# An encoder trunk on one core: the rate at which retention and attention steps are mixed into the weight products

## Chip, cores and metric

One core of a Trainium2 chip runs the kernel, in one launch. The metric is device microseconds of one execution; three runs of the kernel before took 2622.9 to 2623.79 us, median 2623.04 us.

## What is computed

The reference runs an encoder of two layers (DEPTH = 2) over two batches, of 512 and 256 tokens (together T = 768), with the same weights; D_MODEL is 1024. Cut to what matters:

```python
def encoder_layer(x, ...):
    h = rmsnorm(x, norm_mix)
    proj = h @ w_in
    z, xbc, dt_raw, rq, rk, rv, rg, nq, nk, nv, gates = jnp.split(proj, splits, axis=-1)
    ...
    y = bidir_scan(cm, bm, xh * dt_f[..., None], ...)          # the SSD mixer
    o_ssd = rmsnorm(y ... * jax.nn.silu(z), ssd_norm)
    ...
    yr = bidir_scan(q, k, v, la_f, v, la_b)                    # retention, 4 heads
    o_ret = rmsnorm(yr) ... * jax.nn.silu(rg)
    o_na = neighborhood_attention(nq, nk, nv, na_rpb)          # attention, 8 heads
    gates = jax.nn.sigmoid(gates + gate_bias)
    merged = gates[:, :, 0] * (branches[0] @ w_branch[0])      # o_ssd
    for i in range(1, N_BRANCH):
        merged = merged + gates[:, :, i] * (branches[i] @ w_branch[i])   # o_ret, o_na
    x = x + merged @ w_out
    h2 = rmsnorm(x, norm_ffn)
    ...                                                        # gated MLP with a convolution
    return x
```

## The kernel before

**Arithmetic.** Every fp32 value that goes into a large product is split into two parts (`hi` and `lo`, type fp32r), and three matmuls make one product. Weights come by DMA (`wraw`, L197), ScalarE writes `whi` (L206) and VectorE `wlo` (L207). For the projections to nq and nk and to the gates two blocks of 128 output columns are made at once with seven products in place of eight (`pair_products`, L500): each of the seven is four steps of three matmuls with 384 columns (`prod`, L489 to L494), so a pair has 84 matmuls. Its sums are formed on the way from PSUM by ScalarE and VectorE (`soon`, L498) in the tiles `pt`, `pv` and `pg`.

**Stages of a layer.** Norm and the projections for z, dt and xbc; four projections by token tiles (`t_job`) beside which the SSD mixer runs; then sixteen pairs: four for nq and nk (L1178), ten for gate columns in the pool `mix` (L1191) and two more for gates in the pool `br` (L1217). They are called the first four pairs and gate pairs 1 to 12 here. Then the branch products, the output projection and the MLP.

**Side work.** The SSD mixer, retention (`ret`, L924) and attention (`na`, L1052) are Python generators. Each `yield` ends a step; a step holds some loads, some small matmuls and transposes and the ScalarE and VectorE work behind them. `side.pump(p)` adds p to a sum and runs one step for every whole 1.0 in it. `pair_products` calls it six times, after each of its first six products, and the seventh product, put off into the next pair by `pending()`, calls it once more (L565). `t_job` pumps the SSD mixer with 2.7 after each of its 24 token tiles.

- Retention has 27 steps: one of constants, 8 for the chunk states and their sums, and three for each of the six chunks of 128 tokens (scores, output, norm). Its loads `rk`, `rv`, `rqk`, `rgt` share three buffers (`ld2`); the output tile `ro` has one.
- Attention has 56 steps: for each of four head pairs four units of 128 prompt queries and two of sample queries, two steps each (scores with softmax; transposes and values), and two steps that normalise and store. The first step of a head pair loads keys (`kh`, `kl`), for every other head pair also the values (`nv`, many small DMAs), then `q` and `bias`. The scores are `nsc`, the transposed weights `npT`, the output `npo` and `no`.

Each of the two has a pool of its own, opened and closed inside the generator, over the same memory, so attention's tiles wait for retention's. The pool `br` of the last two gate pairs (merged, `oT0h`, `oT0l`, three buffers `g`, two `ot`) is laid over `mix` and attention's pool in the same way; its tiles wait tile by tile. In bytes of a partition, in the order of first use: `mix` 19072; attention `kh` 4096, `kl` 4096, `nv` 7168, `q` 4096, `bias` 4096, `nsb` 6144, `npT` 4096, `no` 2048, and for the sample `kh` 2048, `kl` 2048, `nv` 2048; `br` 24576 + 12288 + 12288, then `g` 3 x 3072, `ot` 2 x 2048.

**Order.** All DMAs are issued by SP, in one queue. The order of instructions on each engine is made when the program is built, by a planner (L1395, `schedule_with_timeline_sim=True`): it takes what is ready by its own reckoning of time, earlier emitted instructions first, and the ones inside `soon` as if they had been emitted 100 earlier. On the chip every engine then goes through its queue in that order. So the place of a `pump` call sets a step's rank, not its exact place.

The lines that the change touches are L1145, where `PUMP` is set, and L1192, where the ten gate pairs pass it on.

Of the kernel before, what the change touches and what calls it, by code (L numbers as in the profile page):

```python
# [283 lines left out]
def body(tc, nc, a, depth=DEPTH):  # L284
# [25 lines left out]
    for n, op in (("ident", OP.is_equal), ("U", OP.is_ge), ("Y", OP.is_le)):  # L310
        m = cst.tile([P, P], F32, name="mask" + n)
# [4 lines left out]
    for n, op in (("V", OP.is_lt), ("W", OP.is_gt)):  # L316
        m = cst.tile([P, P], F32R, name="maskr" + n)
# [254 lines left out]
    def pending():  # L572
        while late:
            late.pop(0)()
# [13 lines left out]
    def layer(l, x_in, prev_x):  # L588
# [5 lines left out]
        m = mctx.enter_context(tc.tile_pool(name=f"mix{l}", bufs=1, reuse_waits="tile"))  # L594
# [547 lines left out]
            nctx.close()  # L1142


        PUMP = 1.6  # L1145

        def pair(pool, tag, bufs, pump, evac):
            vg = [pool.tile([P, T], F32, name=n, tag=tag, bufs=bufs) for n in ("pv", "pg")]
            tmp = pool.tile([P, T], F32, name="pt", tag=tag, bufs=bufs)
            pair_products(*vg, tmp, lambda j: evac(j, vg[j]), pump=pump)  # L1150

        def nq_evac(i, r):

            s = mt([P, T], "nst", "cv", 6)
            src = r[:, :TP].rearrange("p (r c) -> p r c", c=GW)
            if i < 4:
                act(s[:, :TP].rearrange("p (b r c) -> p r b c", b=4, c=16),
                    src.rearrange("p r (b c) -> p r b c", c=16), AF.Copy, scale=0.125)
                act(s[:, TP:T], r[:, TP:T], AF.Copy, scale=0.125)
            else:  # L1160
                act(s[:, 0:64].rearrange("p (r c) -> p r c", c=8), src[:, :, 0:8], AF.Copy)
                act(s[:, 64:448].rearrange("p (b r c) -> p r b c", b=3, c=16),
                    src[:, :, 8:56].rearrange("p r (b c) -> p r b c", c=16), AF.Copy)
                act(s[:, 448:512].rearrange("p (r c) -> p r c", c=8), src[:, :, 56:64], AF.Copy)
                act(s[:, TP:T], r[:, TP:T], AF.Copy)
            hi, lo = (mt([P, T], n, "cv", 6, F32R) for n in ("nhi", "nlo"))
            act(hi, s, AF.Copy)
            tt(lo, s, hi.bitcast(F32), op=OP.subtract)
            for s_ in range(2):
                h, rw = 2 * (i % 4) + s_, slice(s_ * 64, s_ * 64 + 64)  # L1170
                scr, parts = (nq_scr, (hi, lo)) if i < 4 else (nk_scr, (hi, hi))
                for j, part in enumerate(parts):
                    nc.sync.dma_start(scr[h, j * 64:j * 64 + 64], part[rw].bitcast(F32))
            if i >= 4:
                nc.sync.dma_start(nkl_scr[i - 4], lo.bitcast(F32))

        side.add(ret())
        for i in range(0, 8, 2):  # L1178
            pair(m, "cv", 6, PUMP, lambda j, r, i=i: nq_evac(i + j, r))
        side.add(na())  # L1180


        def gates(i, pool, tag, bufs, pump):
            def evac(j, g):
                act(g, g, AF.Tanh, bias=gbh[:, i + j:i + j + 1], scale=0.5)
                nc.sync.dma_start(gate_scr[i + j], g)

            pair(pool, tag, bufs, pump, evac)

        NG1 = 20  # L1190
        for i in range(0, NG1, 2):  # L1191
            gates(i, m, "cv", 6, PUMP)  # L1192
        pending()
        side.drain()
        mctx.close()
# [180 lines left out]
    for l in range(depth):  # L1376
        prev = layer(l, x_in, prev)
        x_in = x_scr
# [20 lines left out]
```

## Time and profile before

| | |
|---|---|
| median of 3 runs | 2623.04 us |
| the profiled execution | 2621.23 us |
| its span, first to last instruction | 2619.5 us |
| TensorE busy | 2560.9 us (98%) |
| VectorE busy | 1906.4 us (73%) |
| ScalarE busy | 1150.0 us (44%) |
| mean granted clock of TensorE | 0.995 |

The stages lie, by the copies of each pair's first product (`pt`, L498): the first four pairs and gate pairs 1 and 2 from 299.3 to 416.8 us, gate pairs 3 to 6 to 528.9, 7 to 9 to 573.1, 10 and 11 to 607.5. In layer 1 the same marks are 1600.2, 1715.2, 1828.4 and 1872.6.

How to read it: TensorE's own ends are modelled and matmuls overlap, so a stretch in which it is busy throughout isn't free of loss by that alone; the spacing of starts tells more. What a wait of another engine costs is seen only where TensorE idles too.

### The profile page before, as it was taken

What the parts mean: (1) busy time and instruction counts of PE and PEld (TensorE: products, weight loads), DVE (VectorE), ACT (ScalarE), POOL (GpSimd) and SP (SyncE); (2) the same over time, 40 slices, a digit from 0 to 9 for tenths busy, and PEclk for the clock granted to TensorE, in tenths of its full rate; (3) what the DMA queues carried; (4) which work ended last, traced back from release to release, by engine and by line L of the source; (5) the groups of instructions that cost most, each with busy time, mean ns of one, the idle gap of its engine ahead of it and who ended that gap; (6) DMA issues with size and microseconds to landing.
All of it is one profiled execution on the core that took longest, in us unless ns stands there. A gap on an engine that the chain in (4) does not pass through costs nothing.

```text
span 2619.5 us, 37552 instructions
## 1 busy us (share of the span) xinstructions
PE 2560.9 (98%) x14290; PEld 2352.9 (90%) x14290; DVE 1906.4 (73%) x3204; ACT 1150.0 (44%) x1946; POOL 86.5 (3%) x130
## 2 busy tenths in 40 slices
PE   8999999999999999999999999999999999999998
PEld 8878898998888999999998789989998899999997
DVE  6748876565658887888867588755656598888887
ACT  5434464643225433333453445655432353333433
POOL 0002100000000000000000011100000000000000
PEclk9999999999999999999999999999999999999999
DMA  7356577736521222222353565786474222222222
GB/s 247 107 167 210 193 229 221 222 130 225 161 87 57 73 73 66 64 73 73 126 181 118 161 224 177 231 238 196 135 229 150 73 81 66 64 65 73 73 65 89
DMA packets 168900, 359.65 MB, mean 137 GB/s; under 512 B 16080, under 2 KB 62480, under 8 KB 168720
## 3 DMA queue, kind: packets, MB, share of 16 engines
q1 hardware_dynamic: 168720, 357.25, 43.3%
q8 instruction: 113, 1.85, 0.3%
q14 instruction: 67, 0.55, 0.1%
HBM read 276.87 MB, written 80.31 MB: 136 GB/s over the span
## 4 chain that ended last, share of the span: by engine, by line
PE 80%; DMA 9%; DVE 5%; ACT 2%; issue 2%; SPq 1%; POOL 1%; DVEq 0%; POOLq 0%; ACTq 0%
PE acc L492 12%; PE acc L493 12%; PE acc L494 12%; PE dn L1343 5%; PE dn L1342 5%; PE dn L1341 5%; PE acc L366 4%; PE acc L368 4%; PE acc L367 4%; PE acc L389 3%; PE acc L388 3%; PE acc L390 3%; DMA cw<-cum_scr 2%; PE wo L390 2%; PE wo L388 2%
## 5 line engine op out<-in xcount | busy, mean ns | idle before, releaser
L206 ACT ACTIVATE whi<-wraw 128x1024 fp32r<-128x1024 f32 (+2 forms) x444 | 432.6, 984 | 644.4 <-DMA wraw<-wp 162.7
L207 DVE TENSOR_TENSOR wlo<-wraw,whi 128x1024 fp32r<-128x1024 f32 (+2 forms) x444 | 499.9, 1131 | 166.5 <-ACT whi L206 163.1
L492 PE MATMUL acc<-hTh,whi 128*128 128x384 f32 x1216 | 413.6, 341 | 5.5 <-DVE pg L498 2.6
L493 PE MATMUL acc<-hTl,whi 128*128 128x384 f32 x1216 | 410.9, 338 | 5.0 <-DVE hTl L435 5.0
L494 PE MATMUL acc<-hTh,wlo 128*128 128x384 f32 x1216 | 409.4, 338 | 0.0
L492 PE MATMUL acc<-Eh,whi 128*128 128x384 f32 x912 | 309.0, 340 | 1.3 <-DVE pv L498 1.3
L494 PE MATMUL acc<-Eh,wlo 128*128 128x384 f32 x912 | 306.9, 338 | 0.0
L493 PE MATMUL acc<-El,whi 128*128 128x384 f32 x912 | 306.9, 337 | 0.0
L492 PEld LDWEIGHTS acc<-hTh,whi 128*128 128x128 f32 x1216 | 229.4, 189 | 9.7 <-ACT pt L498 3.5
L493 PEld LDWEIGHTS acc<-hTl,whi 128*128 128x128 f32 x1216 | 229.4, 189 | 7.5 <-DVE hTl L435 6.0
L494 PEld LDWEIGHTS acc<-hTh,wlo 128*128 128x128 f32 x1216 | 229.0, 188 | 0.4
L389 PE MATMUL acc<-wlo,hTh 128*128 128x512 f32 (+1 forms) x576 | 210.1, 366 | 2.6 <-DVE wlo L207 2.6
L388 PE MATMUL acc<-whi,hTh 128*128 128x512 f32 (+1 forms) x576 | 209.1, 364 | 2.2 <-ACT whi L206 1.5
L390 PE MATMUL acc<-whi,hTl 128*128 128x512 f32 (+1 forms) x576 | 209.3, 365 | 0.0
L1342 PE MATMUL dn<-wlo,ah 128*128 128x512 f32 x528 | 207.6, 393 | 0.0
L1343 PE MATMUL dn<-whi,al 128*128 128x512 f32 x528 | 201.9, 394 | 0.0
L1341 PE MATMUL dn<-whi,ah 128*128 128x512 f32 x528 | 200.5, 393 | 0.0
L492 PEld LDWEIGHTS acc<-Eh,whi 128*128 128x128 f32 x912 | 171.4, 188 | 3.6 <-DVE pv L498 2.7
L366 PE MATMUL acc<-hTh,whi 128*128 128x256 f32 (+1 forms) x512 | 174.1, 340 | 0.0
L1356 DVE TENSOR_TENSOR x<-x,dn 128x512 f32<-128x512 f32 x168 | 111.8, 684 | 85.0 <-PE dn L1343 84.9
L368 PE MATMUL acc<-hTh,wlo 128*128 128x256 f32 (+1 forms) x512 | 173.1, 338 | 0.0
L367 PE MATMUL acc<-hTl,whi 128*128 128x256 f32 (+1 forms) x512 | 173.0, 338 | 0.0
(277 smaller groups left out, 4769.3 us busy)
## 6 DMA issues: line engine op xcount, KB each, us to landing
wraw<-wp SPq DMA_DIRECT2D x284, 512.0 KB
g<-gate_scr SPq DMA_DIRECT2D x48, 384.0 KB
cw<-cum_scr SPq DMA_DIRECT2D x48, 256.0 KB
xt<-xbc_scr SPq DMA_DIRECT2D x20, 512.0 KB
bias<-nab SPq DMA_DIRECT2D x40, 256.0 KB
gate_scr<-pg SPq DMA_DIRECT2D x24, 384.0 KB
gate_scr<-pv SPq DMA_DIRECT2D x24, 384.0 KB
ot<-o_scr SPq DMA_DIRECT2D x36, 256.0 KB
```

What stands on the lines that cost most here:

```text
L206: self.nc.scalar.activation(hi[:, :n], r, AF.Copy)
L207: self.nc.vector.tensor_tensor(lo[:, :n], r, hi[:, :n].bitcast(F32), op=OP.subtract)
L366: mm(o, wh[:, k, :], rh, start=(k == 0), stop=False)
L388: mm(o, hT[0][:, k, ts_], wh[:, cs], start=(k == 0), stop=False)
L389: mm(o, hT[0][:, k, ts_], wl[:, cs], start=False, stop=False)
L390: mm(o, hT[1][:, k, ts_], wh[:, cs], start=False, stop=(k == NK - 1))
L492: mm(o, w[0][:, k, :], r[0][:, k, :], start=first and k == 0, stop=False, skip_group_check=True)
L493: mm(o, w[0][:, k, :], r[1][:, k, :], start=False, stop=False, skip_group_check=True)
L494: mm(o, w[1][:, k, :], r[0][:, k, :], start=False, stop=k == 3, skip_group_check=True)
L1341: mm(ps, ah[:, tsl], wh[:, cs], start=(j == 0), stop=False)
L1342: mm(ps, ah[:, tsl], wl[:, cs], start=False, stop=False)
L1343: mm(ps, al[:, tsl], wh[:, cs], start=False, stop=(j == n - 1))
```

## The change

Two rates replace one. `PUMP` was 1.6 for the first four pairs and for ten gate pairs. Now it is 27/28 for the first four pairs (28 calls, 27 steps of retention) and `PUMP_G` = 56/66 for the ten gate pairs (70 calls, 56 steps of attention). `side.add(ret())`, `side.add(na())`, `side.drain()` and the 0.5 of the last two gate pairs stay where they are.

```diff
-        PUMP = 1.6
+
+        PUMP, PUMP_G = 27 / 28, 56 / 66
...
         NG1 = 20
         for i in range(0, NG1, 2):
-            gates(i, m, "cv", 6, PUMP)
+            gates(i, m, "cv", 6, PUMP_G)
         pending()
         side.drain()
```

## Rows read from the trace of the kernel before

**Rows 1.** The page, busy time and share of the span of each engine.
```profile
PE 2560.9 (98%) x14290; PEld 2352.9 (90%) x14290; DVE 1906.4 (73%) x3204; ACT 1150.0 (44%) x1946; POOL 86.5 (3%) x130
```
**Rows 2.** Windows: length, busy us (instructions) of PE, PEld, DVE, ACT, POOL; clock, DMA, GB/s.
```profile
170.00:299.00 129.00, 129.00 (x646) 108.88 (x646) 97.62 (x201) 55.35 (x120) 23.35 (x20) 0.99 0.56 184
299.30:416.80 117.50, 113.89 (x734) 112.66 (x733) 91.12 (x137) 72.60 (x161) 7.76 (x12) 1.00 0.68 211
416.80:528.90 112.10, 104.57 (x720) 102.15 (x719) 63.89 (x189) 61.90 (x153) 0.00 (x0) 0.98 0.79 230
528.90:573.10 44.20, 44.20 (x255) 44.20 (x254) 28.98 (x40) 19.05 (x25) 0.00 (x0) 1.00 0.36 125
...
1600.20:1715.20 115.00, 112.83 (x729) 111.90 (x728) 90.77 (x137) 72.89 (x161) 8.21 (x12) 1.00 0.70 216
1715.20:1828.40 113.20, 105.87 (x720) 104.12 (x720) 63.99 (x189) 61.85 (x153) 0.00 (x0) 0.97 0.78 228
1828.40:1872.60 44.20, 44.20 (x254) 44.20 (x254) 29.02 (x40) 19.03 (x24) 0.00 (x0) 1.00 0.37 125
```
**Rows 3.** Timeline of TensorE: start, duration; first and last of ten matmuls.
```profile
432.07 0.52 PE L494 MATMUL acc<-Eh,wlo 128*128 128x384 f32 x1
...
434.95 0.34 PE L494 MATMUL acc<-hTh,wlo 128*128 128x384 f32 x1
```
**Rows 4.** Waits of TensorE, 299 to 417: total us, times, longest.
```profile
PE acc L492 <- DVE pg L498: 1.6, 1, 1.6
PE qT L330 <- ACT qd L1005: 1.1, 1, 1.1
PE rst L977 <- DMA rv<-rv_scr: 0.8, 1, 0.8
```
**Rows 5.** The same waits in layer 1, 1600 to 1715.5.
```profile
PE rst L977 <- DMA rv<-rv_scr: 1.0, 1, 1.0
PE acc L492 <- DVE pg L498: 1.0, 1, 1.0
```
**Rows 6.** Waits of TensorE, 417 to 529.
```profile
PE nsc L1101 <- DMA q<-nq_scr: 6.2, 2, 3.7
PE nsc L1101 <- issue: 0.9, 1, 0.9
PE nsc L1101 <- DVE nmx L1109: 0.4, 1, 0.4
```
**Rows 7.** The same in layer 1, 1715.5 to 1829.
```profile
PE nsc L1101 <- DMA q<-nq_scr: 5.1, 2, 3.0
PE nsc L1101 <- DVE no L1130: 0.9, 1, 0.9
PE nsc L1101 <- DVE nmx L1109: 0.7, 1, 0.7
PE nsc L1101 <- DVE wlo L207: 0.7, 1, 0.7
```
**Rows 8.** Timeline of SP's queue where retention ends and attention begins.
```profile
409.91 0.32 SPq L1040 DMA_DIRECT2D o_scr<-ro  x1
...
414.68 9.95 SPq L1070 DMA_DIRECT2D nv<-nv_scr  x10
424.67 0.44 SPq L1092 DMA_DIRECT2D q<-nq_scr  x1
```
**Rows 9.** Timeline of VectorE; in brackets its idle time and what ended it.
```profile
408.43 0.69 DVE L1038 TENSOR_TENSOR ry<-ry,rs 128x512 f32<-128x512 f32 x1 [3.71 <-POOL rs L419]
```
**Rows 10.** Timeline: the last scores of attention and its last store, layer 0.
```profile
513.37 0.28 PE L1102 MATMUL nsc<-kl,q 128*128 128x256 f32 x1
...
526.21 0.38 SPq L1139 DMA_DIRECT2D o_scr<-no  x1
```
**Rows 11.** Timeline: a load of retention and the matmul that waited for it.
```profile
320.49 0.33 SPq L970 DMA_DIRECT2D rv<-rv_scr  x1
...
325.66 0.60 PE L977 MATMUL rst<-rv,kg 128*128 128x128 f32 x3 [0.77 <-DMA rv<-rv_scr]
```

## The prediction

> **What bounds the kernel now.** I read the page first: TensorE is busy 98% of the span [rows 1], so the change can only give back what TensorE loses between its instructions. Then the windows by stage [rows 2]: where the span exceeds TensorE's busy time, it idled. In layer 0 the stretch in which retention runs (299.3 to 416.8) idles 117.50 - 113.89 = 3.6 us, the one in which attention runs (416.8 to 528.9) 112.10 - 104.57 = 7.5 us, and the three gate pairs behind it, which have no side work, idle 0 (44.20 of 44.20: 14.7 us for a pair, 0.175 us for each of its 84 matmuls). Layer 1 has 2.2 us, 7.3 us and 0. Together 20.6 us.
>
> To this comes a slower clock. The granted clock is 0.98 and 0.97 in the two attention stretches and 1.00 in the pairs behind them [rows 2]: behind the longest idle stretch, of 3.7 us, nine matmuls were issued from 432.07 to 434.95, 0.32 us apart, TensorE's lower level (1.2 GHz instead of 2.4) [rows 3]. That cost 2.88 - 9 x 0.175 = 1.3 us; scaled by the missing clock (0.02 to 0.03) layer 1 lost some 2.0 us (an estimate). So the two stretches lose about 24 us in the two layers, 0.9% of the run. No more can be won.
>
> The views of who waited for whom, by stretch, say for what. In retention, layer 0: 1.6 us for `pg` on VectorE, 1.1 us for `qd`, 0.8 us for a load of `rv` [rows 4]; layer 1: 1.0 us for `rv` and 1.0 us for `pg` [rows 5]. In attention, layer 0: 6.2 us for two loads of `q`, the longer 3.7 us, and 1.3 us for small things [rows 6]; layer 1: 5.1 us for two loads of `q`, the longer 3.0 us, and 2.3 us [rows 7].
>
> **The change, part by part.** It adds and removes no instruction. All 14290 matmuls stay, and so do the DMAs; what moves is where the 27 retention and 56 attention steps stand in the order in which the planner takes instructions. There are 28 calls of `side.pump` by the first four pairs and 70 by the ten gate pairs. At 1.6 a call retention was handed out after 17 calls (27/1.6) and attention after 35 (56/1.6, five gate pairs); now it takes 28 and 66. A step is moved with its loads and stores, all on SP's queue, past the weight loads (L197) and the stores of `nq_evac` and the gates (L1186). Waits are added only by tiles that a later pool takes over (below).
>
> *Retention.* Its work already runs past where it was handed out: the store of its last `ro` goes out at 409.91 [rows 8], in gate pair 2, though it was handed out by pair 3 of the first four. Its loads share three buffers (`ld2`), so buffers and not the rate set its pace, and I expect its end at about the same place, 400 to 425. What can go are the waits of two chunks that run close together. The 1.6 us wait for `pg` comes from there: VectorE stood 3.71 us at L1038, waiting for POOL's `rs` [rows 9], with the pair's own instructions queued behind. The `pg` and `qd` waits sum to 1.6 + 1.0 + 1.1 = 3.7 us; at the earliest all go, at the latest none. I take half, **-1.8 us**, as nothing says which. The `rv` waits (1.8 us) belong to the state chunks, whose loads come one buffer ahead before and after: 0.
>
> *The start of attention.* Its pool takes over retention's memory, so its first loads follow retention's end: `kh` behind 409.91, then the small loads of `nv`, of which ten hold SP's queue for 9.95 us, then `q` at 424.67 [rows 8], for which TensorE waits the 3.7 and 3.0 us. The first step issues the same burst wherever it stands, so I keep these 6.7 us and their clock loss: **0**, with -6.7 - 2.3 = -9 us as the good end.
>
> *The rest of attention.* The other waits are 7.5 - 3.7 = 3.8 us in layer 0 and 7.4 - 3.0 = 4.4 us in layer 1, with some 1 us of clock loss 9.2 us. They come with density: twelve loads of `q`, the bias, key and value tiles of a layer go through within some 112 us, and the DMA engines are busy 0.79 there, against 0.36 in the pairs behind [rows 2]. The change spreads the same bytes over 112 + 44 us. The nearest row for even spreading is the SSD stage: its 58 steps are pumped at 2.7 a call over 22 of 24 calls, and behind its start, from 170 to 299, TensorE idles 0 of 129.00 us beside them [rows 2]. But attention starts late (its memory), so about five of its 24 units are handed out by then and run as densely as now. I take three quarters: **-6.9 us**, ends 0 and -9.2.
>
> *The end of attention.* By the tile sizes in the code the pool of the last two gate pairs puts its three `g` buffers where `npT`, `no` and the sample's `kh` and `kl` lie. Before, the last `no` was stored at 526.21 [rows 10], some 47 us ahead of gate pair 10, so that nobody waited for it. Now the last step is handed out at the fourth call of gate pair 10. From the last `nsc` to that store took 526.21 - 513.37 = 12.8 us [rows 10]. That `nsc` is now handed out two products earlier than the last step, and from that step to the copy of gate pair 11's first product (`pt`, L498) are four products, then two more that don't need the copy: eight in all, 8 x 12 x 0.175 = 16.8 us. It just fits, with the landing of the store. I take **+0.8 us** a layer, ends 0 and +6.
>
> *Pairs 7 to 9* lose their quiet: 0 by the SSD row; VectorE is busy 0.66 of them and ScalarE 0.43 [rows 2], which leaves room.
>
> Sum: -1.8 + 0 - 6.9 + 1.6 = **-7.1 us**. The profiled execution took 2621.2 us (span 2619.5 and 1.7 around it), so 2614.1 by it; the median of the runs shown is 2623.0, 1.8 above it, so the median should be **2616 us** (-0.27%).
>
> **The rivals.**
>
> *The rate isn't what these steps wait for (no change).* Retention's pace is set by buffers, the start of attention by the burst, and the backlog behind it runs as before. Then only half of the smaller waits go: (3.7 + 9.2)/4 = 3 us, **2620 us**. For it: retention ended two pairs behind its handing out. Against it: the SSD row. The Trainium skill ("Perfetto Trace Analysis", Optimization Strategy) says that the same gap repeating on the engine that should be saturated can mean that there isn't enough SBUF or PSUM for the next tile. By that rule the gaps are bound to buffers and stay, whatever the rate. The trace agrees for retention's start and for attention's; for the second wait for `q` it shows a busy DMA instead.
>
> *Loads lose their lead (slower).* Handed out at twice the rate, attention's loads went out as soon as a buffer was free, well ahead of their matmuls. Handed out evenly, a unit's `q` is issued next to the matmul that needs it. If the planner thinks loads faster than they are, TensorE meets the matmul early, every time. The nearest row: `rv`, issued at 320.49, let TensorE go on at 325.66 only, after 0.77 us of idling [rows 11]. At 0.8 us for each of 2 x 12 loads that is +19.2, less the -8.7 of the gains: +10.5, **2633.5 us**; it is slower than before from 0.4 us a load on. For it: the waits in [rows 4 to 7] that a load ends. Against it: the SSD stage, which loads its tiles in the same manner and idles 0.
>
> *The tail of attention holds gate pair 11 (about 2627 us).* If attention lags by one unit (some 5 us) more than above, TensorE idles 5 us a layer and loses 1.3 us of clock behind it: +12.6 - 8.7 = +3.9. For it: attention ran one to two gate pairs late before. Against it: that lag came from the density that goes.
>
> *The burst goes too.* If the planner puts the first `nsc` later, -9 comes on top with all of the smaller waits: -22, **2601 us**. Nothing in the trace speaks for it but the room.
>
> **How the numbers follow.** Forecast 0.42 (2611 to 2620), rate without effect 0.28, lead lost 0.14, tail 0.06, burst gone 0.10. About 0.2% (5.2 us) is what a measurement can tell from no change: faster is below 2617.8, slower above 2628.3. Faster: 0.37 of the forecast's 0.42, 0.10 from the burst and 0.03 from the first rival, 0.50. Slower: 0.14, 0.03 of the tail and 0.03 of the first rival with a worse order of queues, 0.20. Same: the remaining 0.30. The range goes from 2604 (most of the burst gone) to 2629 (the tail, and the lower half of the lost lead).
>
> **What would show it.** Right: attention's matmuls reach into gate pair 10; the windows of gate pairs 3 to 6 idle some 5 us a layer instead of 7.5, nearly all of it one wait for the first `q`; gate pairs 7 to 9 take longer and idle under 1 us; the DMA share falls below 0.7 in gate pairs 4 to 6. Wrong: many short waits of `nsc` for `q` (lead lost); a wait of `pt` at gate pair 11 for a store of `no` (tail); retention's end well behind 425, which would push the backlog into the tail; a wait for `pg` or `pv` in pairs that now have none.

## The result, and the profile after

The changed kernel takes 2604.18 us (median of four executions, 2603.32 to 2605.65) where the kernel before takes 2623.41 us beside it: ratio 0.9927, interval 0.9914 to 0.9940. That is 19 us or 0.73% faster. Repeated later on two chips (`after_again` and `after_third` below) the ratio came out as 0.9928 and 0.9921. The forecast was 2616 us. Its sign was right. That the median lies in the range (2604 to 2629) is luck: it does so by 0.2 us, and the interval of the ratio stands for 2601 to 2608 us. The gain is 2.7 times the 7.1 us of the sum.

The profiled execution of the changed kernel took 2605.65 us (span 2603.9), the slowest of its four, against 2621.23 us of before. So the two profiles differ by 15.6 us, not 19. The page's first row says that the work stayed and that its idle time went:

```profile
PE 2560.1 (98%) x14290; PEld 2353.6 (90%) x14290; DVE 1904.2 (73%) x3204; ACT 1153.4 (44%) x1946; POOL 87.8 (3%) x130
```

TensorE is as busy as in [rows 1] within 0.8 us, with the same counts of instructions; the span is 15.6 us shorter.

The windows answer to [rows 2] (same columns). In each layer: first four pairs and gate pairs 1 and 2; gate pairs 3 to 6; 7 to 9, which now have side work too; and, in layer 0, 10 and 11, the first of which has some now.

```profile
299.20:414.80 115.60, 114.33 (x732) 112.07 (x731) 89.94 (x136) 72.64 (x160) 8.66 (x12) 1.00 0.67 209
414.80:501.70 86.90, 85.46 (x570) 84.44 (x570) 54.53 (x138) 47.76 (x107) 0.00 (x0) 1.00 0.84 251
501.70:560.30 58.60, 58.60 (x381) 58.33 (x380) 37.17 (x85) 30.85 (x61) 0.00 (x0) 1.00 0.56 169
560.30:597.60 37.30, 35.91 (x218) 35.06 (x216) 21.51 (x35) 16.43 (x28) 0.00 (x0) 1.00 0.45 148
1586.60:1702.20 115.60, 113.92 (x731) 112.04 (x731) 89.70 (x136) 72.55 (x160) 8.74 (x12) 1.00 0.67 209
1702.20:1796.10 93.90, 88.96 (x571) 87.65 (x570) 55.29 (x139) 48.04 (x108) 0.00 (x0) 0.96 0.81 234
1796.10:1854.70 58.60, 58.60 (x382) 58.34 (x381) 36.81 (x85) 30.87 (x62) 0.00 (x0) 1.00 0.55 166
```

The first number less the second is TensorE's idle time. In layer 0 the retention stretch idles 1.27 us (before 3.61), gate pairs 3 to 6 idle 1.44 us (before 7.53), and 7 to 9 idle 0 as before, though attention now runs beside them and they take 58.60 us instead of 44.20. In layer 1 it is 1.68 us (2.17), 4.94 us (7.33) and 0. So layer 0 gave back three quarters of what it had lost in idle time, and layer 1 of this execution not quite a third.

TensorE's waits in gate pairs 3 to 6 answer to [rows 6, 7] (waiting line, waited for: total us, times, longest). Layer 0 has one left, layer 1 three:

```profile
PE npt L330 <- ACT nsb L1111: 1.3, 1, 1.3
...
PE nsc L1101 <- DMA q<-nq_scr: 2.3, 1, 2.3
PE npo L1124 <- ACT npT L1120: 1.8, 1, 1.8
PE npt L330 <- ACT nsb L1111: 0.9, 1, 0.9
```

The 3.7 us wait for the first `q` of layer 0 is gone here. In the two repeats something is left of it: 1.2 and 0.7 us in layer 0, 0.9 and 1.2 us in layer 1. SP's queue shows how the loads came to be there in time (answers to [rows 8]):

```profile
415.67 0.33 SPq L1040 DMA_DIRECT2D o_scr<-ro  x1
416.10 0.39 SPq L1081 DMA_DIRECT2D kh<-nk_scr  x1
416.54 1.32 SPq L1083 DMA_DIRECT2D kl<-nkl_scr  x2
417.96 3.70 SPq L1070 DMA_DIRECT2D nv<-nv_scr  x6
423.11 0.35 SPq L197 DMA_DIRECT2D wraw<-wp  x1
423.50 1.65 SPq L1070 DMA_DIRECT2D nv<-nv_scr  x3
425.49 0.33 SPq L197 DMA_DIRECT2D wraw<-wp  x1
425.87 1.16 SPq L1070 DMA_DIRECT2D nv<-nv_scr  x2
427.21 0.38 SPq L1092 DMA_DIRECT2D q<-nq_scr  x1
```

Before, the last store of `ro` at 409.91 was followed by `q` at 424.67, 14.8 us later [rows 8]; now 415.67 is followed by 427.21, 11.5 us later. The burst of small `nv` loads is still there, with the same eleven loads. One of them takes SP as long as before (shortest, median and longest in ns; start of the first and of the last in us, before and after):

```profile
L1070 SPq DMA_DIRECT2D nv<-nv_scr x11: 517/527/695, 413.5 to 424.0; - x11
...
L1070 SPq DMA_DIRECT2D nv<-nv_scr x11: 514/527/698, 418.0 to 426.4; - x11
```

So the 9.95 us of [rows 8] are ten issues of half a microsecond and the pauses between them, which the row runs together. It is the pauses that are shorter now. TensorE's timeline shows the first `nsc` right behind a product, without the idle time that stood there before:

```profile
433.52 0.33 PE L492 MATMUL acc<-hTh,whi 128*128 128x384 f32 x1
433.92 0.39 PE L1101 MATMUL nsc<-kh,q 128*128 128x256 f32 x1
```

In layer 1 of this execution it idled 2.27 us for `q` and 1.75 us for `npT`. Behind the first of them the clock fell as in [rows 3]: seven matmuls stand 0.32 us apart instead of 0.175 (the granted clock from 1723 to 1728 is 0.66).

```profile
1723.56 0.38 PE L1101 MATMUL nsc<-kh,q 128*128 128x256 f32 x1 [2.27 <-DMA q<-nq_scr]
...
1725.07 0.52 PE L493 MATMUL acc<-hTl,whi 128*128 128x384 f32 x1
1725.39 0.52 PE L494 MATMUL acc<-hTh,wlo 128*128 128x384 f32 x1
...
1766.51 2.15 PE L1124 MATMUL npo<-nv,npT 128*128 128x64 f32 x16 [1.75 <-ACT npT L1120]
```

The end of attention: the last `no` of layer 0 is stored at 571.50 (before 526.21 [rows 10]), and the copy of gate pair 11's first product, the one that could have had to wait for it, runs at 585.17.

```profile
571.50 0.37 SPq L1139 DMA_DIRECT2D o_scr<-no  x1
```

```profile
585.17 0.47 ACT L498 ACTIVATE pt<-acc 128x384 f32<-128x384 f32 x1
```

The stage, from the copy of the first pair's first product to that of gate pair 12's, went from 308.2 to 298.4 us in layer 0 and from 307.4 to 305.7 us in layer 1. That is 11.5 of the 15.6 us. Some 4 us fell outside, nearly all of them between the two stages, from gate pair 12 of layer 0 to the first pair of layer 1 (992.7 us before, 989.0 now). The change doesn't touch that stretch, and TensorE idles 7.4 us in it where before it idled 10.3.

### The profile page after: what moved, and what is told of

Read it like the earlier page. It is cut to its first block, busy times and chain, and to the rows that moved or that the text cites. A ratio compares the mean times of both kernels' runs of the same rounds, so it can differ in the third digit from the quotient of the medians.

```text
span 2603.9 us, 37538 instructions
## 1 busy us (share of the span) xinstructions
PE 2560.1 (98%) x14290; PEld 2353.6 (90%) x14290; DVE 1904.2 (73%) x3204; ACT 1153.4 (44%) x1946; POOL 87.8 (3%) x130
## 4 chain that ended last, share of the span: by engine, by line
PE 85%; DMA 7%; ACT 3%; DVE 3%; issue 1%; SPq 1%; POOL 0%; DVEq 0%; POOLq 0%; ACTq 0%
PE acc L493 12%; PE acc L492 12%; PE acc L494 12%; PE dn L1344 5%; PE dn L1342 5%; PE dn L1343 5%; PE acc L366 4%; PE acc L368 4%; PE acc L367 4%; PE acc L389 3%; PE acc L388 3%; PE acc L390 3%; PE wo L390 2%; PE wo L388 2%; PE wo L389 2%
## 5 line engine op out<-in xcount | busy, mean ns | idle before, releaser
L494 PE MATMUL acc<-Eh,wlo 128*128 128x384 f32 x912 | 307.4, 338 | 0.0
```

The source lines that it names most:

```text
L494: mm(o, w[1][:, k, :], r[0][:, k, :], start=False, stop=k == 3, skip_group_check=True)
```

## Experiments

All ratios are against the kernel before on the same chip, from five rounds. They were made on three chips, and on each the kernel before spread over 11 to 14 us, so differences of two or three us between kernels mean nothing.

### Each rate alone

`ret_only`: the first four pairs at the new rate, attention at the old one.

```diff
-        PUMP, PUMP_G = 27 / 28, 56 / 66
+        PUMP, PUMP_G = 27 / 28, 1.6
```

> Retention alone is spread (27/28 a call), attention stays at 1.6. Rate theory (attention's density is what costs): the waits of retention go, some 2 us a layer at most, so 2618 to 2622 us. Rival (the later end of retention shifts the first scores to a better place in TensorE's queue, and that is the gain): the wait for the first q goes here too, 2610 to 2614 us.

Measured: 2610.70 us, ratio 0.9954 [0.9937, 0.9970], about 12 us faster. So the rate that I had priced at 1.8 us carries more than half of the whole gain by itself. The time is the rival's; whether its reason holds, a better place in TensorE's queue, is taken up in the next section. Waits of TensorE from 415.3 to 538, layer 0:

```profile
PE nsc L1101 <- DVE wraw L229: 1.4, 1, 1.4
PE nsc L1101 <- DVE wlo L207: 1.0, 1, 1.0
PE npo L1124 <- DMA nv<-nv_scr: 1.0, 2, 0.7
PE nsc L1101 <- DMA q<-nq_scr: 0.6, 1, 0.6
```

The wait for the first `q` is 0.6 us (before 3.7), although not one attention step was respaced. What is left are small waits of several kinds, with attention's rate still at 1.6.

`na_only`: the reverse.

```diff
-        PUMP, PUMP_G = 27 / 28, 56 / 66
+        PUMP, PUMP_G = 1.6, 56 / 66
```

> Attention alone is spread (56/66 a call), retention stays at 1.6. Rate theory: most of the gain, 2606 to 2611 us, with attention's matmuls reaching into gate pair 10. Rival: without retention's shift the wait of 3 to 4 us for the first q stays in both layers, and only the smaller waits go, 2614 to 2618 us.

Measured: 2611.90 us, ratio 0.9950 [0.9937, 0.9964], about 13 us faster, between the two expectations. Waits of layer 0, from 299 to 416.8 and from 416.8 to 568:

```profile
PE acc L492 <- DVE pg L498: 2.2, 1, 2.2
PE acc L492 <- DVE pv L498: 0.6, 1, 0.6
...
PE nsc L1101 <- DVE nmx L1109: 2.3, 1, 2.3
PE nsc L1101 <- DMA bias<-nab: 1.7, 1, 1.7
PE acc L492 <- DVE pg L498: 0.2, 1, 0.2
```

With retention at the old rate its `pg` wait stays in layer 0 [rows 4], and the first `nsc` waits 1.7 us for its loads; in layer 1 it waits 2.4 us for `q`. The second wait for `q` of [rows 6, 7] went; in layer 0 the 2.3 us for `nmx` stand in its place, for which VectorE itself waited for a load of `bias`. The two parts alone make 12 and 13 us, together 19 to 21: they overlap.

### Is it the burst ahead of the first `q`?

The small `nv` loads stand ahead of `q` in SP's queue. This edit puts them behind the first unit's `q` and `bias`; `nv_late_before` has it at the old rates, `nv_late_after` at the new ones.

```diff
-                    v = values(hp, t0 == 0)
                     po = mxbank("npo", "po")
...
+                        if i == 0:
+                            v = values(hp, t0 == 0)
                         sc = mxbank("nsc", "my").rearrange("p (s k) -> p s k", s=2)
```

> The kernel before, with the loads of the value tiles nv issued behind the first q and bias of each head pair instead of ahead of them. If the burst of nv on SP's queue is what the first scores wait for: the waits for q of 3.7 and 3.0 us and the clock loss behind them go, 2613 to 2617 us. If not (the keys or the memory of retention's pool come last): within 2 us of before, or the wait turns up at the first npo instead.

> The changed kernel with the same reordering of the loads. The changed kernel's profile shows 0 and 2.3 us of waiting for the first q in the two layers, so 0 to 4 us are left to win: 2600 to 2604 us. Were evenly spread steps short of lead in their loads, the second head pair's q would show the same and the gain would be larger.

Measured: 2620.72 us, ratio 0.9988 [0.9975, 1.0000], at the old rates; 2611.69 us, ratio 0.9958 [0.9942, 0.9974], at the new ones, which is slower than the changed kernel by itself. Waits of `nv_late_before`, gate pairs 3 to 6 of layer 0 and of layer 1:

```profile
PE nsc L1102 <- DVE nmx L1107: 4.5, 2, 4.3
PE nsc L1102 <- DVE nmx L1110: 1.2, 1, 1.2
...
PE nsc L1102 <- DMA q<-nq_scr: 4.3, 1, 4.3
PE nsc L1102 <- DVE sums L1129: 1.3, 1, 1.3
```

VectorE in layer 0:

```profile
428.58 0.42 DVE L1107 CUSTOM_DVE_ANT_0 nsb<-nsc,bias 128x256 f32<-128x256 f32 x1 [4.84 <-DMA bias<-nab]
```

In its trace `q` is issued 1.8 us behind `kh`, and the first `nsc` idles for nothing. But one wait of 4.3 us comes in its place in both layers: the second `bias` and the second `q` now stand behind the burst (issued at 422.18 and 422.67). In layer 0 TensorE waits for `nmx` on VectorE, and VectorE for that `bias`; in layer 1 the row names the load of `q` itself. So the burst is what the wait is made of, and moving it within the one queue moved the wait to the next unit. With the edit at the new rates one wait for a `q` is 2.1 us in layer 0 and 3.1 us in layer 1. What shortens the wait without moving it is shown by `ret_only`.

### How even must it be?

`after_again` is the changed kernel once more; `rate12` and `rate07` change attention's rate alone.

```diff
-        PUMP, PUMP_G = 27 / 28, 56 / 66
+        PUMP, PUMP_G = 27 / 28, 1.2
```

```diff
-        PUMP, PUMP_G = 27 / 28, 56 / 66
+        PUMP, PUMP_G = 27 / 28, 0.7
```

> The changed kernel once more, beside the others. If its gain is the two parts' gains (12 to 15 us each with retention or attention spread alone) as far as they don't meet in the same wait, 2600 to 2606 us where before takes 2623; if the parts add up in full, 2596 to 2599. Its second layer's profile, with 5 us of waits that the first layer doesn't have, should look different from execution to execution if these are a matter of when loads land, and the same if they are built into the order.

> The changed kernel with attention pumped at 1.2 in place of 56/66 = 0.85 (56 steps in 47 calls, about the first seven gate pairs). Density theory: between retention alone at 1.6 and the changed kernel, 4 to 8 us above the changed kernel in the same call. Rival (what counts is only how the first scores meet their loads): within 2 us of the changed kernel.

> The changed kernel with attention pumped at 0.7: 49 of 56 steps by the pumps, the last seven handed out at once behind gate pair 10. Tail theory: gate pair 11's first copy waits for attention's last tiles, 5 us or more a layer with the slow clock behind it, so 8 to 16 us above the changed kernel. Rival: the planner mixes these steps with gate pair 11's products and nothing waits: within 3 us of the changed kernel.

Measured: `after_again` 2602.64 us, ratio 0.9928 [0.9916, 0.9941]; `rate12` 2610.66 us, 0.9967 [0.9950, 0.9984]; `rate07` 2611.08 us, 0.9960 [0.9947, 0.9972]. Both neighbours of the even rate lose 8 us of its gain. Between 1.6 (`ret_only`, another chip) and 1.2 there is no gain to be seen; it comes on the way from 1.2 to 0.85. Of the 10 us by which the profile of `rate12` is longer than that of `after_again`, only 4.2 lie in the two stages whose side work the rate moves.

What `after_again` shows of layer 1, retention stretch and gate pairs 3 to 6:

```profile
1585.70:1702.20 116.50, 114.08 (x732) 112.07 (x731) 89.73 (x136) 72.91 (x160) 8.47 (x12) 1.00 0.67 209
1702.20:1789.60 87.40, 85.48 (x571) 84.48 (x570) 54.70 (x139) 48.05 (x108) 0.00 (x0) 1.00 0.83 251
```

Here gate pairs 3 to 6 idle 1.9 us at a clock of 1.00, in place of 4.9 us at 0.96 in the first profile of the same program. So what layer 1 kept in that profile is no fixed loss; it differs between executions, and the stage took 299.7 us here. The retention stretch idles 2.4 us, no less than before (2.2).

`rate07`, waits of TensorE in gate pairs 10 and 11, 551.5 to 601.4, and VectorE there:

```profile
PE acc L492 <- DVE pt L498: 1.7, 1, 1.7
PE oT L330 <- DMA ot<-o_scr: 0.8, 1, 0.8
PE acc L492 <- ACT pt L498: 0.6, 1, 0.6
...
586.33 0.42 DVE L1130 TENSOR_TENSOR no<-npo,sums 128x256 f32<-128x256 f32 x1 [5.20 <-DMA o_scr<-no]
```

At 0.7 the pumps hand out 49 of 56 steps, and the last seven are handed out at once behind gate pair 10. VectorE then stands 5.2 us until the store before is through, since `no` has one buffer, and the `pt` that TensorE waits for is queued behind it. The last `no` is stored at 586.78, and the transposes of `oT` wait for `ot` behind it. That is a tail as the rival had it, one step beyond the rate that was chosen, though it comes through VectorE's queue and not through memory that gate pair 11 takes over. It is smaller than the loss: gate pairs 10 and 11 idle 3.7 us here and 2.1 us in layer 1, where the changed kernel idles 1.4 us in each. Where the rest of the 8 us lies is not shown.

`rate12`, waits of TensorE from 413.6 to 549.6:

```profile
PE nsc L1101 <- DMA q<-nq_scr: 1.8, 2, 1.1
PE nsc L1101 <- DVE nmx L1109: 1.2, 1, 1.2
PE npo L1124 <- DMA nv<-nv_scr: 0.4, 1, 0.4
```

Two waits for `q` and one for the maxima: the kinds of [rows 6], shorter.

### The backlog behind retention's end

At the even rate attention's steps are handed out from gate pair 1 on, but none can run before retention's memory is free. By a count of the trace's matmuls, gate pairs 4 to 10 have 78, 116, 40, 46, 33, 47 and 24 matmuls of attention beside them: a backlog in the first two, even only behind it. `late_lead` starts attention ten empty steps later, hands out faster, and puts two empty steps between the first loads and the first scores; `late_only` has the ten alone and the rate 1.0; `late_lead2` and `after_third` are `late_lead` and the changed kernel again, beside `late_only`.

```diff
+            for _ in range(10):
+                yield
...
+                        if hp == u == 0:
+                            yield
+                            yield
...
-        PUMP, PUMP_G = 27 / 28, 56 / 66
+        PUMP, PUMP_G = 27 / 28, 1.1
```

> The changed kernel, with ten empty steps ahead of attention, so that nothing is handed out before retention's memory is free, with two empty steps between the first loads and the first scores, and with 1.1 a call so that it ends where it did (68 steps in 62 calls). If the waits at attention's start come from the planner, which puts the first scores where it thinks the loads have landed, the lead takes them away in both layers, with the dense stretch behind it: 2 to 6 us below the changed kernel. Rival: the planner moves the scores ahead again, or the waits turn up at a denser rest: within 2 us of it.

> The changed kernel with ten empty steps ahead of attention's first, and 1.0 a call, so that its 56 real steps are handed out over calls 11 to 66, one to a call, at the same last call as before; no empty steps between the first loads and the first scores. Theory: what made the run with ten empty steps and two between quicker than the changed kernel (2597.4 against 2602.6 us) was that attention is no longer handed out while retention still runs, so that no backlog runs behind retention's end; the two steps between did nothing. Then this one comes within 3 us of that run, with waits of at most 1.5 us in all in gate pairs 3 to 6. Rival: the gap between first loads and first scores did it; then the wait for the first load of q is 1 us or more in both layers, and the time is that of the changed kernel within 2 us.

> The kernel with ten empty steps ahead of attention and two between its first loads and first scores, once more, beside the other two of this call. If its lead is real it stays 3 to 7 us below the changed kernel on this chip; if it was the spread between executions, the two differ by less than 2 us.

> The changed kernel once more, as the bar for the two others of this call: 18 to 20 us below the kernel before.

Measured: `late_lead` 2597.36 us, ratio 0.9911 [0.9897, 0.9925], the lowest of all; but on another chip `late_lead2` 2602.25 us, 0.9924 [0.9906, 0.9942], `late_only` 2600.57 us, 0.9920 [0.9902, 0.9937], and `after_third` 2601.53 us, 0.9921 [0.9906, 0.9937]. The three stand within 2 us: its lead did not come again. So no version here is shown to beat the changed kernel. In the traces the waits are a little smaller: `late_only` in gate pairs 3 to 6, layer 0 and layer 1:

```profile
PE nsc L1103 <- DMA q<-nq_scr: 0.8, 1, 0.8
PE npt L330 <- ACT nsb L1113: 0.2, 1, 0.2
...
PE npt L330 <- ACT nsb L1113: 0.7, 1, 0.7
PE nsc L1103 <- DMA q<-nq_scr: 0.4, 1, 0.4
```

About 1 us a layer is left to win here, which is below what these runs tell apart. The backlog, which the first of these runs made look like a loss of 5 us, is not one that can be measured.

## Why the prediction was right and wrong

| term, layer 0, us | forecast | measured (idle and clock, first profile) |
|---|---|---|
| retention's stretch | -0.9 (half of -1.8) | 3.61 to 1.27: -2.3 |
| first `q` | 0 | 3.72 and 1.3 of clock to 0.06: -5.0 |
| rest of gate pairs 3 to 6 | -3.45 (half of -6.9) | 3.81 to 1.38: -2.4 |
| gate pairs 7 to 9 | 0 | 0 to 0 |
| end of attention | +0.8 | 1.40 to 1.39: 0 |
| sum | -3.6 | -9.7 (the stage: -9.8) |

The terms add up to the stage's own change, so nothing is left over in layer 0. In layer 1 the stage gained 1.7 us in the first profile and 7.7 us in `after_again`; the idle time of gate pairs 3 to 6 went from 7.33 to 4.94 and to 1.92 us. The table is one execution: over the three profiles of the changed kernel the stage took 298.4, 298.3 and 301.1 us in layer 0 (before 308.2) and 305.7, 299.7 and 298.3 us in layer 1 (before 307.4).

**The step that failed is "The start of attention: 0".** I wrote that the first step issues the same burst wherever it stands, and kept the wait. The burst is the same, and the wait went. `ret_only` shows that retention's rate does most of it: with that one number changed the wait is 0.6 us in layer 0 and the longest wait for `q` is 1.4 us in layer 1. The traces show the distances that changed.

| us | before, layer 0 | before, layer 1 | `na_only`, layer 0 | `ret_only`, layer 0 | after, layer 0 | after, layer 1 |
|---|---|---|---|---|---|---|
| last `rpo` of retention on TensorE to store of `ro` | 7.83 | 7.21 | 8.43 | 6.30 | 6.23 | 6.27 |
| store of `ro` to `kh` | 1.72 | 1.72 | 1.72 | 0.43 | 0.43 | 0.43 |
| `kh` to first `q` | 13.04 | 14.18 | 12.28 | 11.11 | 11.11 | 11.25 |
| issue of `q` to the first `nsc` | 6.13 | 4.00 | 6.14 | 7.15 | 6.71 | 8.78 |
| last `rpo` to TensorE's arrival at the first `nsc` | 25.00 | 24.16 | 26.83 | 24.40 | 24.41 | 24.46 |
| idle ahead of the first `nsc` | 3.72 | 2.95 | 1.73 | 0.60 | 0.06 | 2.27 |
| products in TensorE's order from the last `rpo` to the first `nsc` | 10.75 | 10.75 | 10.75 | 11.5 | 11.5 | 11.5 |

The first four rows are the load's way, the fifth is TensorE's; the idle time is their difference, to 0.02 us in each column. With retention at 27/28 the load's way to the issue of `q` is 4.8 us shorter in layer 0, in three parts. The store of the last `ro` follows its last `rpo` 1.6 us sooner: before, ScalarE had to wait until the store of the `ro` before was through, since `ro` has one buffer and the two chunks ran close together; now it doesn't.

```profile
405.75 0.31 ACT L1035 ACTIVATE ro<-ry 128x128 f32<-128x128 f32 x1 [1.43 <-DMA o_scr<-ro]
...
410.44 0.31 ACT L1035 ACTIVATE ro<-ry 128x128 f32<-128x128 f32 x1
```

Then `kh` follows the store 1.3 us sooner, with no weight load between, and the burst holds `q` 1.9 us less. TensorE's way hardly changed (0.6 us shorter in layer 0, 0.3 us longer in layer 1). The planner does put 0.75 of a product (9 matmuls of 0.175 us, 1.6 us) more ahead of the first scores, but before, TensorE had idled 1.6 us for `pg` on that way, so it arrives no later for it. The rival of `ret_only` is thus right in its time and not in its reason: what moved is when the load goes out, not when TensorE comes to the scores. Against the gain, where TensorE still waits, the load lands later behind its issue (7.15 us in `ret_only` and 8.78 us in layer 1, where before it was 6.13 and 4.00 us), so that some of it is given back, in layer 1 of the first profile most. That these distances changed is shown; why the planner chose so, and why a load lands later, is not. The pauses in the burst were 4.2 us before (layer 0), in which the profile has SP waiting for earlier loads to land (`kl`, `wraw`, `kh`, `nv`); why these took longer there stays open. The 2.27 us that layer 1 had left in the first profile were 0.9 us in `after_again`. I had looked at the last load alone, and asked where it is issued; a wait is the difference of two ways, and I should have followed both from a common point.

**Retention.** That its end would stay between 400 and 425 was right (415.67), and so was the kind of wait that goes; half of it was too little in layer 0. Of the 1.6 us for `pg` and 1.1 for `qd` [rows 4], 0.3 and 0.2 us are left in layer 0. That this comes from the rate is borne out by `na_only`, which keeps 2.2 us for `pg`. In layer 1 no gain is shown: the stretch idles 1.68, 2.42 and 1.10 us in the three profiles, before 2.17. The `rv` waits, which I had kept (0.8 and 1.0 us [rows 4, 5]), are gone in all three, so that 0 was wrong for them; in layer 1 waits for `qd` and `kT` of 0.5 to 0.9 us each came in their place.

**The rest of attention.** That spreading attention takes waits away is borne out by `na_only` and by `rate12` (8 us more than `after_again`, less than half of it in the two stages). That density alone makes them isn't shown apart from what else the planner moved. The signs came: 24 of attention's matmuls stand beside gate pair 10, and gate pairs 7 to 9 are longer and idle 0. In idle time it came out a little under the forecast in layer 0. The step "DMA share below 0.7 in gate pairs 4 to 6" was wrong: it is 0.84 and 0.81 in gate pairs 3 to 6, more than before [rows 2], with the backlog in the first of them; most of the waits went all the same, so this share does not by itself set them. My count of five units handed out by the time that attention starts was right in kind, but the conclusion that they would run "as densely as now", and lose as much, was not.

**Buffers.** The Trainium skill ("Perfetto Trace Analysis", Optimization Strategy) reads a repeating gap on the engine that should be saturated as a possible want of SBUF or PSUM for the next tile. No run here shows that for attention: no buffer was changed, and the gaps went from 7.5 to 1.4 us in layer 0. Single buffers do take part, by the rows of `ro` above and of `no` in `rate07`, and the rate decided whether they were waited for. Whether a second buffer for `ro` at the old rates would have given the same is not tested.

**The rivals.** "The rate isn't what these steps wait for" is wrong by `na_only` and `ret_only`, which each gain 12 us and more. "Loads lose their lead" is wrong at this rate: beside the even part of attention, in gate pairs 7 to 9, TensorE idles 0 of 58.60 us. "The tail" didn't happen at 56/66: the last store is out 13.7 us ahead of the copy that could wait. My +0.8 had left out that the seventh product of gate pair 10, which `pending()` puts behind the ten pairs, and attention's own matmuls lie between too: from pair 10's first copy to pair 11's it takes 24.8 us, with 119 matmuls of products and 24 of attention. `rate07` shows a tail where the rate is one notch lower. "The burst goes too" is what came, at 2601 against a measured 2604; I gave it 0.10, since I saw nothing in the trace for it. Its reason, first scores put later, holds by 0.75 of a product in TensorE's order and by nothing in time (24.4 us from the last `rpo` where it was 25.0). What spoke for its time was the load's way, which the trace of before held: 7.8 us from the last `rpo` to its store, within which lie the 3.71 us that VectorE stood for `rs` [rows 9], and 14.8 us from store to `q`.

**What stays open.** The 4 us that the two profiles differ by outside the stage: the stretch from the copy of layer 0's last pair, in the MLP, to that of layer 1's first pair took 336.1 us in the one profile of the kernel before and 332.0, 333.3 and 331.2 us in the three of the changed one; in the other profiles it took from 331.6 to 336.2 us. So a part of the gain may lie in a stretch whose side work the change leaves as it was, and no run here says why. And why a rate of 1.2 brings nothing over 1.6.

## What to carry over

Side work that is mixed into a busy stream should last as long as the stream, up to the point at which its last step still has its own cover: 0.85 steps a call beat both 1.2 and 0.7 by 8 us. Price a wait as the difference of two ways from one common point: the load's, through what frees its memory and its place in the queue, and that of the engine which needs it. A count of products is not enough for the second, since the idle time among them counts too. A change of rate moves both ways, even for a step whose own loads and work stay the same. And when one wait is removed by shifting a burst within its queue, look for the next load behind the burst: here its unit waited 4.3 us instead.

## What the chip showed that I had not expected

A wait can cost more than its length. Behind 3.72 us of idling TensorE ran nine matmuls at its lower level [rows 3], behind 2.27 us seven, behind 1.75 us four (at 1770 in layer 1 of the changed kernel); in `after_again`, whose longest idle in attention is 1.4 us, no matmul of a product in gate pairs 3 to 6 stands 0.32 us from the next. It isn't so behind every wait: in the kernel before, the second wait for `q` in layer 0 took 2.43 us, and behind it, from 473 to 483, the granted clock is 1.00. So the same program lost 4.9 us of idling in layer 1 at a clock of 0.96 in one execution and 1.9 us at 1.00 in another.

An issue of a small `nv` load takes SP 0.51 to 0.70 us in both kernels, and eleven of them 6.0 to 6.2 us together. What differs is the pauses: from `kh` to `q` it took 13.0 and 14.2 us before and 11.1 and 11.3 us in the changed kernel. So the length of such a burst isn't fixed by its loads.
